# Hybrid attention block on one core: the first weight scale from ScalarE squares, first rows of x issued ahead of the constants

## The chip, the cores and the metric

The kernel runs on one core of one Trainium2 chip. The metric is the device time of one execution in microseconds; the time of a kernel is the median of its runs. PE is TensorE, DVE VectorE, ACT ScalarE, POOL GpSimd, and SP is SyncE, which here only issues transfers. Each engine works through its own queue of instructions in a fixed order.

## The reference

One layer of a residual block on x of 2048 rows by 1024 columns, in float32:

```
u  = rms_norm(x, norm1_w);  p = u @ w_in            # 1024 x 3072
diff q, k, v and sb q, k, v = columns of p
y_A: 4 heads, two softmax maps of normalised q and k, plus rel_bias by distance,
     chunk-causal, p0 - lam * p1, times v, rms_norm (diff_out_norm_w)
     lam = exp(sum(lambda_q1*lambda_k1)) - exp(sum(lambda_q2*lambda_k2)) + 0.2
y_B: 8 heads, stick-breaking attention, strictly causal, rms_norm (sb_out_norm_w)
h  = x + concat(y_A, y_B) @ w_out
out = h + SwiGLU(rms_norm(h, norm2_w); w_gate, w_up, w_down of width 2816)
```

## The kernel before, in words

**Number format.** Products are made in float16 at nearly float32 accuracy: each operand is scaled by a power of two and split into a high and a low half, and three matmuls (high-high, high-low, low-high) give one product. For a weight matrix the scale comes from its largest magnitude (or from sums of squares): a reduction per partition, a product with the identity that carries the 128 partial results across partitions (`across`, L177 and L178), then a few one-element DVE operations that cut the exponent out and write `sW` (L199). `split_weight` (L207 to L216) then makes the high half on ACT, DVE or POOL, whichever its running account of work finds least loaded, and the low half always on DVE (L215), from the raw weights and the high half.

**Work.** Rows of x go in 16 tiles of 128 rows. For each, `fresh` (L598) loads the rows into a `z4` buffer (nine of them), ACT squares and sums them (L220), POOL makes the reciprocal root (L151), DVE multiplies by root and gain (L223). `fresh_t` (L607) transposes the tile on PE in eight 128 x 128 pieces (L594), ACT casts each half of it to float16 (L612), DVE subtracts to get the low half (L613), and SP stores it for the later groups. The projection runs in eight groups of 384 columns (four of the differential heads, four of the stick-breaking ones); group 0 uses the tiles as they are made, the others read them back. Per group and tile PE makes 24 matmuls of 384 columns into `pj` (L320): eight blocks of 128 rows of weights, three matmuls each. `load_w` (L279) loads, scales and splits the weights of a group; for group 0 it is called at the start, for each other group at the ninth tile of the group before.

**Constants.** `gq`, `gk`, the four lambda vectors and the output gains (`mgain`) come by transfers on ACT's queue (L139, L680, L682) and are worked on by DVE in small steps (L650 to L690). `build_bias` (L625) makes the table of relative biases of four heads: a one-hot product on PE for each (L633), a copy on DVE (L635), a store and a skewed reload on POOL's queue (L637, L640), a last multiplication (L641).

**What sets the order.** The program is written as one sequence; a scheduler then fixes each engine's order by a timeline that it works out when the kernel is built, with priorities by part (`high_priority`), so a change at one place can move instructions anywhere behind it. Attention of group g runs beside the projection of group g+1. After attention come the output projection and the FFN, whose products run on PE almost without a break.

**Reading the names.** A reduction of the first weights is L187, the square of a later group's weights L184. In rows of order and profile, `wst` is a group's raw weights, `w` its two halves, `z` any row buffer, `xtr` a transposed half tile in PSUM, `xt` its float16 form, `wsc` the product that carries the scale across partitions, `xss` and `xrs` the sum of squares and reciprocal root of a row tile.

## Time and profile before

| | |
|---|---|
| median of 3 runs (2746.8 to 2756.92) | 2750.41 us |
| the profiled execution | 2752.86 us, span 2751.1 us |
| mean granted TensorE clock | 0.968 |
| PE busy | 2489.3 us, 90% of the span |
| DVE, ACT, POOL busy | 1967.9, 1357.8, 1428.8 us |
| first projection matmul | 25.40 us |

A row of the timeline gives start and length in us, engine, source line, operation, written from read tiles, shapes, how often in a row, and in brackets the engine's idle time before it with what ended that. Lengths in a chain overlap a little, so steps from start to start are the better measure. `SPq` and `ACTq` are the issuing of transfers by those engines. A single-pass PE transpose is counted once, a float32 matmul as two.

### The profile page before, as it was taken

What the parts mean: (1) busy time and instruction counts of PE and PEld (TensorE: products, weight loads), DVE (VectorE), ACT (ScalarE), POOL (GpSimd) and SP (SyncE); (2) the same over time, 40 slices, a digit from 0 to 9 for tenths busy, and PEclk for the clock granted to TensorE, in tenths of its full rate; (3) what the DMA queues carried; (4) which work ended last, traced back from release to release, by engine and by line L of the source; (5) the groups of instructions that cost most, each with busy time, mean ns of one, the idle gap of its engine ahead of it and who ended that gap; (6) DMA issues with size and microseconds to landing.
All of it is one profiled execution on the core that took longest, in us unless ns stands there. A gap on an engine that the chain in (4) does not pass through costs nothing.

```text
span 2751.1 us, 45381 instructions
## 1 busy us (share of the span) xinstructions
PE 2489.3 (90%) x17084; PEld 1411.3 (51%) x17084; DVE 1967.9 (72%) x3752; ACT 1357.8 (49%) x2539; POOL 1428.8 (52%) x1002
## 2 busy tenths in 40 slices
PE   7998989898878786788988899999999999999999
PEld 4655555555545453457775444444444444444444
DVE  6888879797989989977655878777776644443434
ACT  4665656566878778765644535353342211121120
POOL 2567767665454545546655656555654322232322
PEclk9999999999999997989999999999999999999999
DMA  7788787879999988987887665656657845535532
GB/s 231 197 163 182 151 191 160 180 167 206 196 209 194 199 177 150 205 186 202 211 247 271 235 232 192 225 204 213 237 200 280 339 150 187 210 131 199 188 118 93
DMA packets 646829, 543.52 MB, mean 198 GB/s; under 512 B 506368, under 2 KB 573952, under 8 KB 636368
## 3 DMA queue, kind: packets, MB, share of 16 engines
q1 hardware_dynamic: 644784, 538.53, 71.7%
q8 instruction: 134, 2.20, 0.3%
q0 software_dynamic: 512, 1.36, 0.2%
q14 instruction: 87, 0.71, 0.1%
q10 hardware_dynamic: 1312, 0.72, 0.1%
HBM read 261.08 MB, written 147.32 MB: 148 GB/s over the span
## 4 chain that ended last, share of the span: by engine, by line
PE 33%; DVE 7%; DMA 6%; POOL 3%; issue 3%; ACT 2%; SPq 0%; DVEq 0%; POOLq 0%; ACTq 0%
PE pd L1034 12%; PE pm L934 7%; PE pd L934 6%; PE pa L934 5%; DVE wd L215 2%; DMA stages<-in_w_down_dram 1%; DMA aT<-s 1%; POOL stages L98 1%; PE po L761 1%; POOL s L98 1%; DMA X<-xcd 1%; DMA stages<-in_w_up_dram 1%; DVE wu L215 1%; DVE cg L98 1%; DVE cg L999 1%
## 5 line engine op out<-in xcount | busy, mean ns | idle before, releaser
L98 POOL TENSOR_TENSOR s<-z,s 128x1024 f16<-128x1024 f32 (+7 forms) x288 | 473.5, 1652 | 339.3 <-ACT s L89 300.5
L320 PE MATMUL pj<-w,xt 128*128 128x384 f16 x3072 | 574.4, 335 | 28.1 <-DVE st L330 12.6
L320 PEld LDWEIGHTS <-xt 128*128 128x128 f16 x3072 | 300.7, 100 | 239.6 <-issue 39.4
L448 PE MATMUL sc<-kT,qT 128*128 128x512 f16 (+3 forms) x1280 | 346.8, 361 | 72.8 <-DVE z L558 32.1
L557 DVE TENSOR_TENSOR_SCAN z<-z,sc 128x512 f32<-128x512 f32 (+3 forms) x320 | 355.5, 1113 | 70.7 <-ACT sc L555 68.5
L1034 PE MATMUL pd<-wd,act 128*128 128x512 f16 x1764 | 392.9, 380 | 8.5 <-DVE cu L968 7.0
L458 PE MATMUL yp<-v,aT 128*128 128x64 f16 (+1 forms) x4896 | 281.0, 208 | 79.1 <-DMA aT<-s 78.4
L458 PEld LDWEIGHTS <-aT 128*128 128x128 f16 x4896 | 244.9, 102 | 169.1 <-DMA aT<-s 107.7
L934 PEld LDWEIGHTS <-wg 128*128 128x128 f16 x1848 | 181.3, 98 | 224.4 <-issue 10.9
L934 PEld LDWEIGHTS <-wu 128*128 128x128 f16 x1848 | 181.7, 98 | 220.8 <-issue 8.2
L98 POOL TENSOR_TENSOR act<-cg,act 128x512 f16<-128x512 f32 x109 | 150.4, 1390 | 259.4 <-ACT act L993 259.4
L1034 PEld LDWEIGHTS <-act 128*128 128x128 f16 x1764 | 172.8, 98 | 217.0 <-issue 10.9
L89 ACT CAST s<-z 128x384 f16<-128x384 f32 (+7 forms) x216 | 170.5, 790 | 157.8 <-DMA aT<-s 65.4
L98 POOL TENSOR_TENSOR stages<-stages 128x512 f32<-128x512 f32 x97 | 170.2, 1755 | 120.2 <-DVE wg L215 43.2
L98 POOL TENSOR_TENSOR hs<-hs,cu 128x512 f32<-128x512 f32 x102 | 132.6, 1306 | 162.0 <-DVE hs L1040 60.2
L554 ACT ACTIVATE z<-sc,c 128x512 f32<-128x512 f32 (+3 forms) x320 | 203.5, 636 | 10.7 <-PE sc L448 5.9
L558 DVE TENSOR_TENSOR z<-sc,z 128x512 f32<-128x512 f32 (+3 forms) x320 | 193.3, 606 | 8.1
L555 ACT ACTIVATE sc<-sc,c 128x512 f32<-128x512 f32 (+3 forms) x320 | 195.7, 611 | 0.0
L761 PE MATMUL po<-wo,mt 128*128 128x256 f16 x1536 | 182.4, 277 | 11.4 <-DVE xf L764 6.8
L993 ACT CAST act<-cg 128x512 f16<-128x512 f32 x126 | 76.8, 616 | 231.3 <-DVE cg L999 193.4
L1040 DVE SCALAR_TENSOR_TENSOR hs<-pd,c,hs 128x512 f32<-128x512 f32 x144 | 106.2, 747 | 116.8 <-PE pd L1034 104.5
L934 PE MATMUL pm<-X,wu 128*128 128x512 f16 x792 | 179.3, 379 | 1.8 <-ACT cg L979 1.7
(241 smaller groups left out, 4109.9 us busy)
## 6 DMA issues: line engine op xcount, KB each, us to landing
xt<-xs SPq DMA_DIRECT2D x112, 512.0 KB, 4.3
hs<-hd SPq DMA_DIRECT2D x72, 512.0 KB, 4.4
hd<-hs SPq DMA_DIRECT2D x56, 512.0 KB, 6.1
split<-wg SPq DMA_DIRECT2D x11, 1792.0 KB, 6.9
split<-wu SPq DMA_DIRECT2D x11, 1792.0 KB, 6.7
split<-wd SPq DMA_DIRECT2D x11, 1792.0 KB, 6.8
wg<-split SPq DMA_DIRECT2D x11, 1792.0 KB, 7.4
wd<-split SPq DMA_DIRECT2D x11, 1792.0 KB, 9.1
```

The costliest lines, as they stand in the source:

```text
L89: ACT.copy(dst, src)
L98: (DVE if e == "D" else POOL).tensor_tensor(dst, a_, b_, op)
L320: PE.matmul(pj[:, :384], lhsT=xv[:, xi, kt, :], rhs=G["w"][:, wi, kt, :], start=n == 0, stop=n == 23)
L448: PE.matmul(sc[:, : 128 * w].rearrange("p (t n) -> p t n", n=P), lhsT=G["q"][i // 4][:, 2 - 2 * o + m, i % 4, :], rhs=G["k"][q][:, m, 0:w, ...
L458: PE.matmul(yp[:, y0 : y0 + wd], lhsT=aT[:, a_, :], rhs=v[:, v_ : v_ + wd], start=start and j == 0 and q == 0, stop=stop and j == nb - 1 a ...
L554: ACT.activation(om[:, lo:hi], sc[:, :w], AF.Sigmoid, scale=G["nkz"][:])
L555: ACT.activation(sc[:, :w], sc[:, :w], AF.Sigmoid, scale=G["kz"][:])
L557: DVE.tensor_tensor_scan(ov, ov, sc[:, :w], om[:, hi : hi + 1], op0=ALU.mult, op1=ALU.bypass)
L558: DVE.tensor_tensor(be[:, lo:hi], sc[:, :w], om[:, lo + 1 : hi + 1], ALU.mult)
L761: PE.matmul(po[:, sl], lhsT=mt[:, kt, P * xi : P * xi + P], rhs=wos[2 * h + n][wi][:, kt, :], start=q == 0, stop=q == 23)
L934: PE.matmul(ps_[:].rearrange("p (t n) -> p t n", n=P), lhsT=wv[:, wo, wi, 128 * kt : 128 * kt + 128], rhs=X[xo][:, :, xi, kt, :], start=st ...
L1034: PE.matmul(po[:], lhsT=act[:, ao, xi, 128 * j : 128 * j + 128], rhs=W["d"][:, wo, wi, :], start=start and u == 0 and q == 0, stop=u == nu ...
```

## The change

Five edits, all in the start of the kernel and in `load_w`:

1. The scale of group 0's weights comes from three ACT squares with an accumulated sum, one for each third of the columns as it lands, in place of three DVE reductions of magnitudes (L187). DVE adds the three sums, one product carries them across partitions (instead of three).
2. Later groups' weights are squared in four pieces of 768 elements instead of one of 3072.
3. Loads of x, gain and weights, the norm of the gain row, row tile 0 and group 0's load are given high priority; row tile 1 is fed inside group 0's split, behind the scale.
4. High halves of group 0 are no longer made on DVE (`"AP"` for `"ADP"`); later groups' may also go to ACT.
5. The work on the constants is put in four functions that are emitted behind the first four projected tiles, queued behind the split and behind that tile's last projection matmul; the bias tables' buffers come from the tags `s16` and `aT` in place of `z4`. Group 1's load queues behind a copy of the ninth tile on ACT.

```diff
+            with tc.high_priority(4000):
+                SP.dma_start(xpre[0][:, :D], x[:P, :])
+                ACT.dma_start(w1[:, :D], a["norm1_w"].partition_broadcast(P))
+                st0 = fetch_w(0)
...
-            def load_w(g, st=None):
+            def load_w(g, st=None, hook=None):
...
+                junk = w16[:, : KT * 384].bitcast(BF16).rearrange("p (k n) -> p k n", k=KT)
                 if first:
-                    sW = weight_scale([st[:, :, 128 * j : 128 * j + 128] for j in range(3)], rW[:], pW[:], pt)
+                    pieces = [(st[:, :, 128 * j : 128 * j + 128], junk[:, :, 128 * j : 128 * j + 128]) for j in range(3)]
                 else:
-                    sW = weight_scale([st[:].rearrange("p k n -> p (k n)")], rW[:], pW[:], pt, w16[:, : KT * 384].bitcast(mybir.dt.bfloat16))
+                    pieces = [(st[:, 2 * j : 2 * j + 2, :], junk[:, 2 * j : 2 * j + 2, :]) for j in range(4)]
...
+                for j, (pc, jk) in enumerate(pieces):
+                    ACT.activation(jk, pc, AF.Square, accum_out=m0[:, j : j + 1])
+                note("A", 2900)
+                ms1 = sm.tile([P, 1], F32, tag="m1", name=nm("ms1"))
+                DVE.tensor_reduce(ms1[:], m0[:, : len(pieces)], op=ALU.add, axis=AX.X)
+                marks["scale"] = scale_end(lambda m: across(m, pt, [ms1[:]]), rW[:], pW[:], True, sW)
                 kn = 1 if first else 4
                 for k in range(0, KT, kn):
+                    if k == 3 and first:
+                        hook()
                     ks = slice(k, k + kn)
-                    split_weight(wv[:, 0, ks, :], wv[:, 1, ks, :], st[:, ks, :], 384 * kn, sW, "ADP" if first else "P")
+                    marks["split"] = split_weight(wv[:, 0, ks, :], wv[:, 1, ks, :], st[:, ks, :], 384 * kn, sW, "AP")
...
-                oh, rb = z4(), z4()
+                oh, rb = (s16p.tile([P, 2048], F16, tag="s16", bufs=SB, name=nm("oh"))[:].bitcast(F32) for _ in range(2))
...
-                    bt = z4()
+                    bt = sp.tile([P, 16, P], F16, tag="aT", bufs=AB, name=nm("bt"))[:].rearrange("p k n -> p (k n)").bitcast(F32)
...
+            later = (qk_gains, lambdas, build_bias, mix_gains)
...
-                        if g == 0 and t == 0:
-                            build_bias()
+                        if g == 0 and t < len(later):
+                            with tc.issue_after(first_split.ins), tc.issue_after(marks["proj"].ins):
+                                later[t]()
...
-                            Gs[g + 1] = load_w(g + 1)
+                            with tc.issue_after(marks["raw"].ins) if g == 0 else nullcontext():
+                                Gs[g + 1] = load_w(g + 1)
```

Line numbers of the changed kernel are a little higher: L627 and L628 there are L612 and L613 of before, L216 is L215, L299 the new square, L302 the new sum of its results.

ACT's queue from the first row tile's square on, before (`z_105`, `z_106` and `z_107` are the rows of tiles 0, 1 and 2; `wst_110` group 0's weights, `wst_813` group 1's):

```order
L220 ACTIVATE z_126,xss_127<-z_105 128x1024
L139 DMA lambda_q_238<-in_lambda_q_dram 128x64
L139 DMA lambda_k_240<-in_lambda_k_dram 128x64
L680 DMA c_265<-in_diff_out_norm_w_dram 128x1
L682 DMA c_265<-in_sb_out_norm_w_dram 64x1 x2
L220 ACTIVATE z_133,xss_134<-z_106 128x1024
L612 CAST xt_140<-xtr_141 128x512
L612 CAST xt_140<-xtr_148 128x512
```

and now:

```order
L220 ACTIVATE z_126,xss_127<-z_105 128x1024
L299 ACTIVATE w_149,m_154<-wst_110 128x8x128
L139 DMA lambda_q_225<-in_lambda_q_dram 128x64
L139 DMA lambda_k_227<-in_lambda_k_dram 128x64
L677 DMA c_229<-in_diff_out_norm_w_dram 128x1
L679 DMA c_229<-in_sb_out_norm_w_dram 64x1 x2
L299 ACTIVATE w_149,m_154<-wst_110 128x8x128 x2
L220 ACTIVATE z_174,xss_175<-z_106 128x1024
L627 CAST xt_133<-xtr_134 128x512
L627 CAST xt_133<-xtr_141 128x512
```

One square of the weights stands ahead of the remaining issues, two behind them and ahead of row tile 1's square and tile 0's casts.

DVE's queue around the first scale, before (`wsc` is what the product across partitions left; `sW` the scale):

```order
L178 TENSOR_REDUCE m_181<-wsc_175 128x1
L664 TENSOR_REDUCE c_242<-lambda_q_234 128x1
L654 TENSOR_SCALAR c_222<-c_222 128x1
L658 TENSOR_SCALAR c_230<-c_223 128x1
L663 TENSOR_TENSOR lambda_q_238<-lambda_q_238,lambda_k_240 128x64
L683 TENSOR_SCALAR c_265<-c_265 128x1
L133 TENSOR_SCALAR m_181<-m_181 128x1
L223 SCALAR_TENSOR_TENSOR z_133<-z_106,xrs_136,z_104 128x1024
```

and now, from the sum of the squares to the scale:

```order
L302 TENSOR_REDUCE ms_158<-m_154 128x1
L628 TENSOR_TENSOR xt_133<-xtr_134,xt_133 128x512
L178 TENSOR_REDUCE m_160<-wsc_152 128x1
L628 TENSOR_TENSOR xt_133<-xtr_141,xt_133 128x512
L195 TENSOR_SCALAR m_160<-m_160 128x1
L170 TENSOR_SCALAR c_151<-m_160 128x1
L171 TENSOR_SCALAR c_151<-c_151 128x1
L172 TENSOR_SCALAR c_150<-c_151 128x1
L130 TENSOR_SCALAR c_209<-c_151,c_118 128x1
L199 TENSOR_SCALAR sW_153<-c_150 128x1
```

The constants' operations and row tile 1's gain product are out of the scale's way; the two subtractions for tile 0 (`xt_133`) stand in it.

DVE's queue now from the split's second part to the end of tile 1's subtraction (`z_174`, `z_289`, `z_357` and `z_445` are the normalised rows of tiles 1 to 4, `xt_181` is tile 1 for the matmuls):

```order
L223 SCALAR_TENSOR_TENSOR z_174<-z_106,xrs_177,z_104 128x1024
L216 SCALAR_TENSOR_TENSOR w_149<-wst_110,sW_153,w_149 128x384 x3
L150 TENSOR_SCALAR xrs_449<-xss_447 128x1
L216 SCALAR_TENSOR_TENSOR w_149<-wst_110,sW_153,w_149 128x384
L684 TENSOR_TENSOR gk<-gk,gq 128x64
L694 TENSOR_TENSOR lambda_q_221<-lambda_q_221,lambda_k_223 128x64
L694 TENSOR_TENSOR lambda_q_225<-lambda_q_225,lambda_k_227 128x64
L645 COPY oh_410<-oh_410 32x512
L708 TENSOR_SCALAR c_229<-c_229 128x1
L223 SCALAR_TENSOR_TENSOR z_289<-z_107,xrs_292,z_104 128x1024
L223 SCALAR_TENSOR_TENSOR z_357<-z_356,xrs_361,z_104 128x1024
L628 TENSOR_TENSOR xt_181<-xtr_182,xt_181 128x512
```

Behind that stand L223 of `z_445`, two small reductions and tile 1's second half. Before, tile 1's subtractions stood ahead of the split. On PE, the first projection matmuls now have eight transposes (tile 0) ahead of them instead of sixteen transposes and two bias products; from there on transposes stand up to four tiles ahead of the projection, where before they stood one tile ahead.

95 lines of the change are left out of this document (51 added, 44 removed).

## The prediction

> **What bounds the kernel now.** I read the page's 40 slices first, then the busy times by stage, then the timeline of the first 46 us, where the change puts its instructions. The view by stage gives the busy us of PE, PEld, DVE, ACT and POOL (instruction counts in brackets), the granted TensorE clock, the DMA share and GB/s:
>
> ```profile
> 0.00:25.40 25.40, 9.66 (x29) 6.33 (x30) 15.68 (x53) 8.88 (x15) 6.33 (x15) 1.00 0.61 187
> ...
> 39.90:43.40 3.50, 0.01 (x1) 0.00 (x0) 0.44 (x2) 3.50 (x8) 0.92 (x2) 1.00 0.69 260
> 43.40:105.00 61.60, 58.48 (x373) 38.59 (x374) 50.69 (x83) 36.59 (x79) 27.50 (x24) 0.94 0.70 220
> ```
> ```profile
> 105.00:1550.00 1445.00, 1236.35 (x11175) 823.66 (x11174) 1185.14 (x2603) 950.52 (x1971) 859.53 (x582) 0.95 0.86 194
> ```
> ```profile
> 1550.00:2751.00 1201.00, 1170.31 (x5451) 535.58 (x5449) 708.24 (x988) 356.46 (x467) 529.98 (x372) 0.99 0.56 200
> ```
>
> PE is the engine to watch. It loses 15.7 us ahead of its first projection, 3.5 us at 40 us, 3.1 us in the rest of the first projection pass, 208.7 us in the attention stages and 30.7 us in the FFN. The change works on the first three losses, 22.3 us in all. From about 1600 us on every engine has the same order in both programs, so that an early lead passes through there and nothing new arises.
>
> The start, on PE:
>
> ```profile
> 16.32 0.79 PE L177 MATMUL wsc<-id,m 128*128 128x128 f32 x2 [1.49 <-DVE c L133]
> 17.58 1.97 PE L594 MATMUL xtr<-id,z 128*128 128x128 f32 x8 [0.46 <-DVE z L223]
> ...
> 25.40 2.45 PE L320 MATMUL pj<-w,xt 128*128 128x384 f16 x7
> ...
> 33.80 0.91 PE L633 MATMUL bt<-z,z 32*128 32x384 f32 x2
> 34.64 4.40 PE L320 MATMUL pj<-w,xt 128*128 128x384 f16 x26
> 38.87 1.04 PE L594 MATMUL xtr<-id,z 128*128 128x128 f32 x8
> 43.45 2.82 PE L320 MATMUL pj<-w,xt 128*128 128x384 f16 x8 [3.54 <-ACT xt L612]
> ```
>
> A projection matmul steps by (38.87 - 34.64) / 26 = 0.163 us, a transpose takes 1.04 / 8 = 0.13 us, one bias table's product 34.64 - 33.80 = 0.84 us. At 43.45 us two row tiles are projected (48 matmuls) and three transposed (24). The 3.54 us stall is ACT's: it waits for group 1's weights and squares them whole, ahead of the casts:
>
> ```profile
> 38.59 2.76 ACT L184 ACTIVATE w<-wst 128x3072 bf16<-128x3072 f32 x1 [3.14 <-DMA wst<-in_w_in_dram]
> ...
> 41.35 0.36 ACT L341 ACTIVATE raw<-pj 128x256 f32<-128x256 f32 x1
> ...
> 42.81 1.07 ACT L612 CAST xt<-xtr 128x512 f16<-128x512 f32 x2
> ```
>
> **Step 1: the first scale, some 1.1 us earlier.** Three DVE reductions of the weights go, three ACT squares come. On ACT, the issues of 12 to 15 us and two squares:
>
> ```profile
> 13.84 1.17 ACTq L682 DMA_DIRECT2D c<-in_sb_out_norm_w_dram  x2
> ```
> ```profile
> 44.03 1.08 ACT L220 ACTIVATE z<-z 128x1024 f32<-128x1024 f32 x1
> ...
> 45.07 1.08 ACT L220 ACTIVATE z<-z 128x1024 f32<-128x1024 f32 x1
> ```
>
> The new order puts the second and third square behind the sb_out transfers, whose issue ends at 15.01 us. A square of 1024 elements with its accumulator read steps by 45.07 - 44.03 = 1.04 us, so the sums are there at 17.1. But DVE's new queue holds the subtraction for tile 0's first half ahead of the scale's last reduction, and ACT makes that half's cast only after squaring row tile 1 (18.1) and casting for 1.07 / 2 us (18.7). The DVE rows for what follows:
>
> ```profile
> 16.25 1.27 DVE L223 SCALAR_TENSOR_TENSOR z<-z,xrs,z 128x1024 f32<-128x1024 f32 x1
> ```
> ```profile
> 22.36 0.67 DVE L613 TENSOR_TENSOR xt<-xtr,xt 128x512 f16<-128x512 f32 x1
> ...
> 29.14 0.27 DVE L178 TENSOR_REDUCE c<-msc 128x1 f32<-128x128 f32 x1
> ...
> 29.45 0.56 DVE L635 COPY z<-bt 128x384 f32<-128x384 f32 x1
> 29.93 0.14 DVE L133 TENSOR_SCALAR c<-c 128x1 f32<-128x1 f32 x1
> ...
> 30.11 0.15 DVE L134 TENSOR_SCALAR c<-c 128x1 int32<-128x1 int32 x1
> ```
>
> A subtraction of 0.67 us, a reduction of 0.27, the second subtraction and five dependent small operations at 30.11 - 29.93 = 0.18 us: 18.7 + 2.5 = 21.2 is the scale's end. Before, by the first row here, it was 22.1:
>
> ```profile
> 21.99 0.13 DVE L199 TENSOR_SCALAR sW<-c 128x1 f32<-128x1 f32 x1
> ```
> ```profile
> 22.22 3.08 POOL L214 TENSOR_SCALAR w<-wst,sW 128x384 f16<-128x384 f32 x4 [3.73 <-DVE sW L199]
> ```
> ```profile
> 23.80 1.13 DVE L215 SCALAR_TENSOR_TENSOR w<-wst,sW,w 128x384 f16<-128x384 f32 x2
> ```
> ```profile
> 23.92 1.38 POOL L214 TENSOR_SCALAR w<-wst,sW 128x384 f16<-128x384 f32 x1
> ```
> ```profile
> 28.61 0.60 DVE L215 SCALAR_TENSOR_TENSOR w<-wst,sW,w 128x384 f16<-128x384 f32 x1
> ```
>
> Row tile 0 itself is ready earlier, but PE can do nothing with it ahead of the weights.
>
> **Step 2: the split, some 1.7 us of loss.** Before, POOL and ACT made four high halves each; now POOL makes seven. POOL's first three took (23.92 - 22.22) / 3 = 0.57 us each. Its fourth took 1.38 us beside two low halves on DVE, and ended 0.37 us behind them. So I let POOL's high halves take turns with DVE's low halves and with the gain product of row tile 1 (L223) that now stands among them: 7 x 0.57 + 8 x 0.57 + 1.27 = 9.8 us, ending at 31.0. Were they side by side, DVE alone would set the end: 0.8 for the first high half, 8 x 0.57 and 1.27 give 6.6 us and 27.8. Before it was 29.2. I take 31.0, as the 1.38 us row is the nearest one, and keep 27.8 for the range.
>
> The Trainium skill speaks against this edit: "SBUF — State Buffer", section "SBUF: two separate sides", says that a VectorE operation with two SBUF inputs and a GpSimd operation that reads SBUF exclude each other on a shared port pair, for the whole instruction. The rows above agree (1.38 against 0.57 us); by that rule the split ends at the later of my two values, without it at the earlier.
>
> **Step 3: tiles 0 to 2.** Behind the last low half DVE's new queue holds five constant operations (1.2 us), the L223 of row tiles 2 and 3, the first half of tile 1's subtraction, another L223, two small reductions (0.4) and the second half: 31.0 + 1.2 + 3 x 1.27 + 2 x 0.67 + 0.4 = 37.7. PE needs that half from tile 1's fifth block on and has ten matmuls left, so tile 1 ends at 39.3. Before it ended at about 39.0: up to here nothing is won.
>
> What is won lies behind. No square of group 1 stands on ACT here any more (they come some eight row tiles later, when those weights have long landed), so that the 3.54 us go; and at 39.3 PE has done 36 transposes where it had done 24. Lead: (43.45 - 39.3) + 12 x 0.13 = 5.7 us. Against it stand the four bias products and the mgain one (as the 0.79 us row), which lay ahead of 43 us and now come later: 4 x 0.84 + 0.8 = 4.2. That leaves 1.5 us.
>
> **Step 4: rest of the pass.** PE's waits between 43 and 105 us (engine, tile, line, releaser: total, times, longest):
>
> ```profile
> PE wsc L177 <- ACT raw L341: 1.6, 1, 1.6
> PE xtr L594 <- DVE xt L613: 0.8, 1, 0.8
> PE pj L320 <- DVE m L178: 0.6, 1, 0.6
> ```
>
> All are at the spot where group 1's scale is formed; it moves behind the ninth tile's projection, with its sum formed beforehand. Between none and all of 3.0 us go; I take two thirds, 2 us. The constants that move into this stage (four bias copies of 0.56 us, some twenty small operations of 0.14) cost DVE 5 us, under 61.6 - 50.7 = 10.9 us of its idle time. If that cover fails, PE waits for DVE and these 2 us are lost with the lead.
>
> **Step 5: later groups.** Each group's one square, 41.35 - 38.59 = 2.76 us to the next, becomes four of 768 elements. The nearest row is an exponential of that size, which steps by 0.92 us:
>
> ```profile
> 127.24 0.93 ACT L497 ACTIVATE z<-z,ng 128x768 f32<-128x768 f32 x1
> ...
> 128.16 0.92 ACT L497 ACTIVATE z<-z,ng 128x768 f32<-128x768 f32 x1
> ```
>
> ACT gains 4 x 0.92 - 2.76 = 0.9 us of work a group, 6.4 us over seven. It is busy 950.5 of the 1445 us of these stages, so I cost this at nothing; without that cover it is 6.4 us. Of the six sets that fall there four stand in one piece on ACT, so that little comes in between. One large high half moves from POOL to ACT: nothing.
>
> **The sum.** -1.5 - 2 = -3.5 us on the profiled execution (2752.86 us for a span of 2751.1, and 2.5 us above the median of 2750.41). On the median: **2747 us**. With the side-by-side split (31.0 - 27.8 = 3.2) and all of step 4's waits it is -1.5 - 3.2 - 3.0 = -7.7; with the DVE cover failing, 0.
>
> **The rivals.** Up to 1550 us all orders were drawn anew, mostly by a few places, and the trace cannot price that exactly. PE's longest waits there:
>
> ```profile
> PE yp L458 <- DMA aT<-s: 78.4, 66, 4.2
> PE sc L448 <- DVE z L558: 32.1, 34, 2.0
> ```
>
> - *Slower, through SP's queue.* PE's value products wait for transposing transfers, which SP issues in order; the first such moves stand at the first batches (k's transpose ahead of q's, an attention transpose ahead of a q one). The place is the 78.4 us row: a fifth more there is +15.7, and 2747 becomes 2762. From 5% more on, the lead is gone. For it: 66 waits, each hanging on one neighbour in a queue. Against: the moves are short and go both ways.
> - *Faster.* The lead of 7.7 us, and 15% less of the same wait (-12): 2750.4 - 7.7 - 12 = 2731.
> - *The change doesn't do what it says.* The scale comes no earlier, as the squares stand behind ACT's issues and the cast, and DVE's constants eat steps 3 and 4: 2750. For it: step 3 wins nothing up to tile 1.
>
> **How the numbers follow.** Forecast 0.50 (2747, own range 2743 to 2750); no lead 0.16 (2750); slower 0.16 (2762); faster 0.18 (2731). A measurement of this kernel can tell about 0.5%, 13.8 us, from no change. Below 2736.7 lies the faster rival alone, 0.18; above 2764.2 half of the slower one, 0.08; the rest, 0.74, is no change. The range reaches to both outer cases and leaves out half of each, 0.17: 2731 to 2760.
>
> **What would show it.** Step 1: two squares starting at 15 us on ACT, and the scale at 21 us on DVE. Step 2: POOL's high halves at 1.1 to 1.4 us each between DVE's low ones, the last of which ends at 31 us. Step 3: tile 1's end at 39 us with no 3.5 us gap behind it. Step 4: the first attention scores some 4 us earlier than in this row:
>
> ```profile
> 104.73 0.34 DVE L487 CUSTOM_DVE_ANT_0 z<-sc,bias,c 128x128 f32<-128x128 f32 x1
> ```
>
> Rival: PE's wait for aT well off 78 us. I would be wrong if the split ended by 28 us, if the transposes that now stand up to four tiles ahead held PE up for late rows of x, or if the attention stages differed by more than 10 us.

## The result, and the profile after

| | before | changed |
|---|---|---|
| median, run beside each other | 2752.18 us (2744.71 to 2756.92, 22 runs) | 2756.15 us (2752.87 to 2762.55, 22 runs) |
| ratio of changed to before | | 1.0020, 95% interval 1.0012 to 1.0028 |
| the same on another occasion | | 1.0025, 1.0015 to 1.0035 |
| the profiled execution | span 2751.1 us | span 2759.8 us |
| mean granted TensorE clock | 0.968 | 0.968 |

The changed kernel is slower by 0.2%, some 5 to 7 us, where 3.5 us less were forecast. The profiled execution of the changed kernel lies 5.4 us over its median, so that the two profiles differ by more (8.7 us) than the kernels do. Up to 45 us its profile does nearly what the forecast says. DVE's timeline, from the scale on:

```profile
21.12 0.15 DVE L199 TENSOR_SCALAR sW<-c 128x1 f32<-128x1 f32 x1
...
24.31 0.94 DVE L216 SCALAR_TENSOR_TENSOR w<-wst,sW,w 128x384 f16<-128x384 f32 x1
25.18 1.60 DVE L223 SCALAR_TENSOR_TENSOR z<-z,xrs,z 128x1024 f32<-128x1024 f32 x1
26.70 0.94 DVE L216 SCALAR_TENSOR_TENSOR w<-wst,sW,w 128x384 f16<-128x384 f32 x1
27.56 0.93 DVE L216 SCALAR_TENSOR_TENSOR w<-wst,sW,w 128x384 f16<-128x384 f32 x1
28.42 0.60 DVE L216 SCALAR_TENSOR_TENSOR w<-wst,sW,w 128x384 f16<-128x384 f32 x1
...
29.01 0.60 DVE L216 SCALAR_TENSOR_TENSOR w<-wst,sW,w 128x384 f16<-128x384 f32 x1
```

The scale is there at 21.3 us (22.1 before), and the last low half ends at 29.6 (29.2 before, 31.0 forecast). POOL's high halves beside that:

```profile
21.45 2.01 POOL L214 TENSOR_SCALAR w<-wst,sW 128x384 f16<-128x384 f32 x3 [11.89 <-DVE c L130]
23.43 0.85 POOL L151 TENSOR_TENSOR xrs<-xrs,mh 128x1 f32<-128x1 f32 x1
24.27 0.58 POOL L214 TENSOR_SCALAR w<-wst,sW 128x384 f16<-128x384 f32 x1
24.83 0.88 POOL L214 TENSOR_SCALAR w<-wst,sW 128x384 f16<-128x384 f32 x1
25.68 1.55 POOL L214 TENSOR_SCALAR w<-wst,sW 128x384 f16<-128x384 f32 x1
27.21 0.88 POOL L214 TENSOR_SCALAR w<-wst,sW 128x384 f16<-128x384 f32 x1
```

The two engines take turns here. A POOL half takes 0.58 us alone or first, and 0.88, 1.55 and 0.88 us where it starts beside a low half, the gain product (L223) and another low half. DVE's low half takes 0.60 us alone and 0.94 or 0.93 us beside POOL, the gain product 1.60 us where it took 1.27 alone. Read by their ends, each of POOL's last three halves ends 0.45 us after the DVE instruction that it met; each of DVE's three low halves beside them ends 0.40 us after POOL's half, and the gain product 1.07 us after (25.71 to 26.78). The second profile of the changed kernel has the same steps.

PE's timeline from the last matmuls of row tile 1 on has no gap at the place of the old 3.54 us, and row tile 3's projection starts at 45.2 us, where the two profiles of the kernel before have 50.0 and 51.8:

```profile
36.34 2.11 PE L335 MATMUL pj<-w,xt 128*128 128x384 f16 x12
38.29 0.60 PE L609 MATMUL xtr<-id,z 128*128 128x128 f32 x4
38.72 1.46 PE L335 MATMUL pj<-w,xt 128*128 128x384 f16 x8
...
43.70 1.55 PE L648 MATMUL bt<-oh,oh 32*128 32x384 f32 x4
45.19 0.99 PE L335 MATMUL pj<-w,xt 128*128 128x384 f16 x5
```

At 50 us PE has made 88 projection products and 60 transposes (73 and 32 before). At 80 us it has made 209 and 96 (213 and 96). The whole lead goes in these 30 us, in which PE is idle for 4.7 us and was idle for none before. The waits of PE between 43 and 105 us (engine, tile, line, releaser: total, times, longest):

```profile
PE xtr L609 <- DVE xt L628: 4.2, 3, 1.7
PE wsc L177 <- DVE ms L302: 2.2, 1, 2.2
PE pj L335 <- DVE c L178: 1.3, 1, 1.3
```

That is 7.7 us, where before had 6.5 us with the 3.5 us gap, and 3.0 without it (in a second profile of each, 7.2 us against 10.5 with a gap of 7.7, so 2.8 without it). The transposes wait for PSUM that DVE has not read out yet, and POOL's timeline shows why DVE is late:

```profile
55.35 0.59 POOL L655 DMA_DIRECT2D bias<-bd  x1 [2.49 <-DMA bd<-bt]
55.93 0.54 POOL L652 DMA_DIRECT2D bd<-bt  x1
57.50 0.54 POOL L655 DMA_DIRECT2D bias<-bd  x1 [1.03 <-DMA bd<-bt]
58.06 0.57 POOL L151 TENSOR_TENSOR xrs<-xrs,mh 128x1 f32<-128x1 f32 x1
61.60 0.59 POOL L655 DMA_DIRECT2D bias<-bd  x1 [2.97 <-DVE xrs L150]
62.20 0.56 POOL L151 TENSOR_TENSOR xrs<-xrs,mh 128x1 f32<-128x1 f32 x1
```

POOL issues the bias tables' transfers, and reading a table back waits for the landing of its write. POOL stands still meanwhile, and the power that finishes a row tile's reciprocal root stands behind it. DVE's next gain products then wait:

```profile
58.66 1.28 DVE L223 SCALAR_TENSOR_TENSOR z<-z,xrs,z 128x1024 f32<-128x1024 f32 x1 [2.20 <-POOL xrs L151]
...
62.80 1.28 DVE L223 SCALAR_TENSOR_TENSOR z<-z,xrs,z 128x1024 f32<-128x1024 f32 x1 [1.67 <-POOL xrs L151]
```

and PE with them, 1.68 us at 64.9 and 1.75 us at 71.7. Before, the tables were read back between 28 and 42 us, and the power behind the last of these reads, at 43.0 us, waited for DVE and not for the read. The rest goes at group 1's scale: its squares, held behind the ninth tile's copy, stand on ACT from 82.9 to 86.3 us, and PE waits 2.21 us for their sum.

From 105 us to the end of the projections PE's longest wait is the one for the attention's transposing transfers, as before:

```profile
PE yp L473 <- DMA aT<-s: 87.4, 78, 3.4
PE sc L463 <- DVE z L573: 30.2, 41, 1.5
```

The first row was 78.4 us, in 66 times. To place the loss, marks that every kernel here has were read from the timelines: the first attention score on PE, the first of the 320 scans on DVE (the stick-breaking half begins), the 241st, the last. Two profiles of one program differ too, which shows how much a difference has to be:

| us | first score | first scan | 241st | last | 241st to last | last scan to end |
|---|---|---|---|---|---|---|
| before | 104.3 | 614.4 | 1135.2 | 1400.3 | 265.1 | 1350.8 |
| before, second profile | 106.4 | 613.8 | 1135.4 | 1396.8 | 261.4 | 1349.6 |
| changed | 106.4 | 614.4 | 1134.4 | 1404.6 | 270.2 | 1355.2 |
| changed, second profile | 108.8 | 617.3 | 1137.2 | 1404.7 | 267.5 | 1352.5 |

At the 241st scan the kernels are level within what repeats differ. In the last group's attention, with the output projection beginning under it, the changed kernel takes 268.9 us on the mean of its two profiles, the other 263.3: 5.6 us more. The repeats of one kernel differ by 2.7 and 3.7 us there, so that two profiles of each make this the likely place and don't prove it. Behind the last scan the changed kernel's profiles take another 3.7 us more on the mean (repeats 2.7 and 1.2 us apart); no wait was found for these. PE's waits from the 241st to the last scan, changed kernel:

```profile
PE yp L473 <- DMA aT<-s: 17.9, 10, 3.4
PE osc L177 <- ACT wo L184: 5.0, 3, 2.7
PE po L789 <- DVE xrs L150: 3.3, 2, 2.2
```

and kernel before:

```profile
PE yp L458 <- DMA aT<-s: 12.5, 13, 2.2
PE po L761 <- DVE xf L764: 6.8, 6, 3.3
PE sc L448 <- DVE z L558: 5.3, 6, 1.7
```

5.4 us more for aT, and 5.0 us at a place that was free of waits: the product that carries the output weights' scale across partitions (`osc`) comes up in PE's queue before the squares that it needs are done. The second profiles have the same: 17.3 us against 11.7 for aT, 4.1 against none at `osc`. No edit touches these operations; their places in the queues were drawn anew.

### The profile page after: what moved, and what is told of

The parts are those of the page before. It is cut to its first block, busy times and chain, and to the rows that moved or that the text cites. A ratio compares the mean times of both kernels' runs of the same rounds, so it can differ in the third digit from the quotient of the medians.

```text
span 2759.8 us, 45460 instructions
## 1 busy us (share of the span) xinstructions
PE 2485.6 (90%) x17080; PEld 1408.3 (51%) x17080; DVE 1979.1 (72%) x3761; ACT 1363.4 (49%) x2580; POOL 1438.7 (52%) x1006
## 4 chain that ended last, share of the span: by engine, by line
PE 35%; DVE 8%; DMA 5%; issue 3%; POOL 3%; ACT 2%; SPq 0%; DVEq 0%; POOLq 0%; ACTq 0%
PE pd L1062 14%; PE pm L962 8%; PE pd L962 6%; PE pa L962 5%; DVE wd L216 2%; PE po L789 2%; DMA aT<-s 1%; DMA stages<-in_w_down_dram 1%; DVE wu L216 1%; DMA X<-xcd 1%; POOL stages L98 1%; POOL s L98 1%; DVE cg L1027 1%; DVE cg L98 1%; DVE z L572 1%
## 5 line engine op out<-in xcount | busy, mean ns | idle before, releaser
L335 PE MATMUL pj<-w,xt 128*128 128x384 f16 x3072 | 569.2, 333 | 17.9 <-ACT raw L356 6.0
L473 PE MATMUL yp<-v,aT 128*128 128x64 f16 (+1 forms) x4896 | 283.1, 209 | 88.4 <-DMA aT<-s 87.4
L789 PE MATMUL po<-wo,mt 128*128 128x256 f16 x1536 | 185.7, 280 | 11.7 <-DVE c L172 3.8
L1068 DVE SCALAR_TENSOR_TENSOR hs<-pd,c,hs 128x512 f32<-128x512 f32 x144 | 106.3, 748 | 115.5 <-PE pd L1062 109.4
L962 PE MATMUL pm<-X,wg 128*128 128x512 f16 x792 | 181.6, 383 | 1.2 <-ACT bx L1137 1.2
```

Source lines behind the costliest of these rows:

```text
L335: marks["proj"] = PE.matmul(pj[:, :384], lhsT=xv[:, xi, kt, :], rhs=G["w"][:, wi, kt, :], start=n == 0, stop=n == 23)
L473: PE.matmul(yp[:, y0 : y0 + wd], lhsT=aT[:, a_, :], rhs=v[:, v_ : v_ + wd], start=start and j == 0 and q == 0, stop=stop and j == nb - 1 a ...
L789: PE.matmul(po[:, sl], lhsT=mt[:, kt, P * xi : P * xi + P], rhs=wos[2 * h + n][wi][:, kt, :], start=q == 0, stop=q == 23)
L962: PE.matmul(ps_[:].rearrange("p (t n) -> p t n", n=P), lhsT=wv[:, wo, wi, 128 * kt : 128 * kt + 128], rhs=X[xo][:, :, xi, kt, :], start=st ...
```

## The experiments

All ratios are to the kernel before, run beside the kernel in question. The theories in the expectations: **A**, the deferred constants eat the lead; **B**, the redrawn order decides; **C**, the longer squares in pieces are on the path; **D**, the front wins and other parts lose it; **E**, queues of engines that issue transfers hold the first pass up, and what is won there reaches the end.

| | ratio, 95% interval | first score | first scan | last scan | 241st to last |
|---|---|---|---|---|---|
| e1 constants early | 1.0034, 1.0022 to 1.0045 | 109.2 | 618.8 | 1402.9 | 264.2 |
| e2 one square later | 1.0050, 1.0038 to 1.0063 | 108.1 | 619.7 | 1407.9 | 267.1 |
| e3 only pieces | 1.0028, 1.0016 to 1.0040 | 108.6 | 615.0 | 1402.7 | 263.2 |
| e4 redraw only | 0.9998, 0.9987 to 1.0009 | 107.2 | 626.5 | 1404.1 | 255.5 |
| e6 front only | 1.0027, 1.0016 to 1.0038 | 111.1 | 618.2 | 1397.5 | 255.4 |
| e7 deferral only | 1.0023, 1.0013 to 1.0032 | 112.0 | 623.2 | 1396.5 | 253.4 |
| e8 bias buffers only | 0.9987, 0.9974 to 1.0000 | 104.1 | 609.7 | 1388.7 | 257.1 |
| e9 bias reads held | 1.0031, 1.0019 to 1.0043 | 106.3 | 610.4 | 1404.0 | 267.2 |
| e10 group 1 not held | 1.0020, 1.0007 to 1.0032 | 107.4 | 617.0 | 1398.4 | 254.5 |
| e11 changed, redrawn | 1.0057, 1.0043 to 1.0072 | 107.1 | 626.7 | 1406.9 | 254.6 |
| e12 before again | 1.0001, 0.9992 to 1.0010 | 106.4 | 613.8 | 1396.8 | 261.4 |
| e13 start delayed | 1.0018, 1.0009 to 1.0028 | 109.0 | 615.4 | 1396.9 | 262.6 |
| e14 group 1 later | 0.9994, 0.9983 to 1.0004 | 94.7 | 611.7 | 1384.8 | 251.6 |
| e15 wo earlier | 1.0009, 0.9999 to 1.0019 | 106.0 | 610.6 | 1395.1 | 263.2 |
| e16 bias buffers again | 0.9978, 0.9967 to 0.9989 | 104.5 | 618.4 | 1397.7 | 255.2 |
| e17 front and buffers | 0.9969, 0.9955 to 0.9982 | 105.2 | 613.6 | 1386.3 | 254.7 |
| e18 both repairs | 1.0016, 1.0001 to 1.0030 | 94.2 | 610.8 | 1399.7 | 261.9 |

**e1**, from the changed kernel:

```diff
-            later = (qk_gains, lambdas, build_bias, mix_gains)
+            for part in (qk_gains, lambdas, mix_gains):
+                part()
...
-                        if g == 0 and t < len(later):
-                            with tc.issue_after(first_split.ins), tc.issue_after(marks["proj"].ins):
-                                later[t]()
+                        if g == 0 and t == 0:
+                            build_bias()
```

> The changed kernel, with its deferred constants and bias tables put back to where the kernel before has them (the small constant products straight behind group 0's weights, the bias tables behind the first row tile's projection); all else stays changed. In the changed kernel PE waits 7.7 us between 43 and 105 us (transposes for DVE's subtraction 4.2, group 1's scale product 2.2, the mgain slot 1.3), and a lead of 15 projection products and 28 transposes at 50 us is gone at 80. Theory A (the deferred work fills DVE, POOL and the projection's slots in the first pass, and that eats the lead): PE's waits in 43 to 105 us fall to 4 us or less, the first attention scores start 3 to 4 us before the changed kernel's 106.4 us, and the time is 3 to 4 us under the changed kernel's, about the kernel before's 2752. Theory B (the time is made by how the order from 1130 us on was redrawn, where the changed kernel loses 5 us): the time stays at the changed kernel's, some 4 to 5 us over the kernel before, whatever the first scores do.

A falls as it was put: PE's waits between 43 and 105 us are 11.4 us, not 4 or less, and nothing is won in the time. Tile 8 starts at 75.4 us, 2 us sooner, and then another queue takes over. SP's timeline:

```profile
70.33 1.34 SPq L387 DMA_TRANSPOSE qT<-st  x1
...
72.34 1.57 SPq L387 DMA_TRANSPOSE kT<-st  x1
74.02 1.43 SPq L389 DMA_DIRECT2D qT<-qT  x2
75.54 0.54 SPq L629 DMA_DIRECT2D xs<-xt  x1
76.12 0.45 SPq L618 DMA_DIRECT2D z<-in_x_dram  x1
```

The last row tile's load is issued behind the first q and k transposes, and ACT, in order too, stands still for it:

```profile
82.04 1.06 ACT L220 ACTIVATE z<-z 128x1024 f32<-128x1024 f32 x1 [3.80 <-DMA z<-in_x_dram]
```

Tile 9 starts at 90.1 us, 3 us later than in the changed kernel.

**e2**, from the changed kernel:

```diff
-                    pieces = [(st[:, 2 * j : 2 * j + 2, :], junk[:, 2 * j : 2 * j + 2, :]) for j in range(4)]
+                    pieces = [(st[:].rearrange("p k n -> p (k n)"), w16[:, : KT * 384].bitcast(BF16))]
```

> The changed kernel, with one square over all 3072 elements for the weights of groups 1 to 7, as before, in place of four pieces of 768. Theory C (the pieces' longer work, 3.4 us by the rows at 82.9 to 86.3 us against 2.76 for one square, lies on the path of every group): 5 to 6 us under the changed kernel, at or below the kernel before's 2752. Theories A and B: no gain that follows the number of groups; the first pass as in the changed kernel (first scores at 106 us give or take 1), and the time within 3 us of the changed kernel's 2756, but for what a new order draws at 1130 to 1280 us.

**e3** does the converse: the kernel before with only the four pieces and DVE's sum of them, for groups 1 to 7.

```diff
-                    sW = weight_scale([st[:].rearrange("p k n -> p (k n)")], rW[:], pW[:], pt, w16[:, : KT * 384].bitcast(mybir.dt.bfloat16))
...
+                    for j in range(4):
+                        ACT.activation(junk[:, 2 * j : 2 * j + 2, :], st[:, 2 * j : 2 * j + 2, :], AF.Square, accum_out=m0[:, j : j + 1])
...
+                    DVE.tensor_reduce(ms1[:], m0[:], op=ALU.add, axis=AX.X)
```

> The kernel before, with only the squares of groups 1 to 7 in four pieces and their sum formed by DVE. Theory C: 5 to 6 us over the kernel before, so 1.002 of it. Theory A: no change at the start, and the time of the kernel before. Theory B: the order of all engines up to 1500 us is redrawn by this edit too, so the time may move by some 5 us either way, with the difference arising at few places and not by an equal step in each group.

Taking the pieces out costs, and putting them in costs: 1.0050 against the changed kernel's 1.0020 to 1.0025, and 1.0028 against 1. C would need opposite signs. It falls as a term that adds up; what both edits share is a redrawn order.

**e4**, from the kernel before, changes only the planner's tally:

```diff
+            note("A", 300)
             ahead, nq, nx = [], [], [0, 0]
```

> The kernel before, with 300 ns added once to the planner's tally of ACT ahead of the first row tiles: no instruction is added or left out but one or two small ones that change their engine, and the order of every engine is redrawn (403 places on DVE against 518 in the changed kernel). Theory B: a time off the kernel before's by 2 to 8 us, of either sign. Theories A and C: the time of the kernel before within 2 us, since none of the work that they blame is there.

The time stays, where B had 2 to 8 us. Inside, the profile is 12 us later at the first scan and takes 6 to 10 us less from the 241st to the last. How much of that is the order isn't shown: this profile is of an execution of 2759.66 us, 11 us over the run's median of 2748.50, and two profiles of another program (e8 and e16) are 8.7 us apart at the first scan. What e4 does show is that not every draw changes the time.

**e5 and e12** are the two kernels unaltered, for the second profiles of the table above; e5's ratio is the 1.0025.

> The changed kernel once more, unaltered, as the yardstick for the other three on the same chip and for how far two profiled executions of one program differ, stage by stage. All theories: 1.001 to 1.003 of the kernel before. If the 5 us that the first profile loses between 1130 and 1300 us belong to the order (theory B), they stand here too; if they are the chance of one execution, they don't.

> The kernel before, unaltered, for a second profile of it: how far two executions of one program differ, stage by stage, next to the 1 to 3 us between the two profiles of the changed kernel. All theories: ratio 1.000, first scores within 1 us of 104.7 us. Theory B needs the stage from 1135 to 1400 us to come out within 3 us of the first profile's 265 us; where it doesn't, the 4 to 5 us lost there by the changed kernel are within chance.

The loss stands in the second profile of the changed kernel too (267.5 us). But the second profile of the kernel before has 261.4 us, 3.7 off the first one's 265.1: by the condition set here, the 4 to 5 us lost in this stage are within chance. What both profiles of each kernel do share are the waits for aT and at `osc`.

**e6**, from the changed kernel, leaves only the front (edits 1 and 3 and the `"AP"` of group 0); it is e17 below with the old buffers:

```diff
-                oh, rb = (s16p.tile([P, 2048], F16, tag="s16", bufs=SB, name=nm("oh"))[:].bitcast(F32) for _ in range(2))
+                oh, rb = z4(), z4()
...
-                    bt = sp.tile([P, 16, P], F16, tag="aT", bufs=AB, name=nm("bt"))[:].rearrange("p k n -> p (k n)").bitcast(F32)
+                    bt = z4()
```

**e7**, from the kernel before, makes only the deferral:

```diff
-                        if g == 0 and t == 0:
-                            build_bias()
+                        if g == 0 and t < len(later):
+                            with tc.issue_after(first_split.ins), tc.issue_after(marks["proj"].ins):
+                                later[t]()
```

**e8**, from the kernel before, makes only the new buffers, and **e16** is e8 once more:

```diff
-                oh, rb = z4(), z4()
+                oh, rb = (s16p.tile([P, 2048], F16, tag="s16", bufs=SB, name=nm("oh"))[:].bitcast(F32) for _ in range(2))
...
-                    bt = z4()
+                    bt = sp.tile([P, 16, P], F16, tag="aT", bufs=AB, name=nm("bt"))[:].rearrange("p k n -> p (k n)").bitcast(F32)
```

Expected of e6, e7, e8 and e16, in this order:

> The changed kernel reduced to its front: group 0's weights and row tile 0 ahead of all else, their scale from ScalarE squares, high halves on ACT and POOL, the second row tile within the split. The constants, bias tables, their buffers, and the later groups' weights are as in the kernel before. Theory D (the front is worth what it wins, and the other parts lose it again): tile 1 of the projection done at 39 us or before, the first attention scores 2 to 4 us before the kernel before's 104.7 us, and 0.998 to 0.999 of its time. Theory B (the lead doesn't last, since the order behind it is redrawn): a lead at 50 us, nothing left of it by 130 us, and a time between the kernel before's and 8 us over it.

> The kernel before, with only the constant products and the bias tables held back to the first four row tiles' projections. Theory A's remainder (deferral by itself costs DVE and PE in the first pass): 2 to 4 us over the kernel before, first scores 2 us later than 104.7 us. Theory D: the same, since the deferral is one of the parts that lose. Theory B: as the other redrawn orders, 0 to 8 us over the kernel before, without a link to the first scores.

> The kernel before, with only the bias tables' buffers changed (from the pool of row buffers to those of the attention's fp16 scores and transposes); no operation is added, dropped or moved in the program text. Theories A and D: the kernel before's time within 2 us. Theory B: the order is redrawn by this as well (512 places on DVE), and the time is 0 to 8 us over the kernel before.

> The kernel before with only the bias tables' buffers changed, once more, on another occasion. Its first ratio was 0.9987, from 0.9974 to 1.0000. Theory B: 0.998 to 1.000 again, as a property of its order, with the profile within 3 us of its first one up to 1300 us. If the first result was chance: 0.9995 to 1.001.

Front alone and deferral alone are each as slow as the whole change, with first scores 5 to 8 us late. D falls in this form. The buffers alone are a gain, twice, which no theory had for e8. In the kernel before, the bias build takes six of the nine row buffers (two inputs and four tables). The order there puts the fourth row tile's load on SP behind group 1's weights, which wait for the end of the split, and the next two loads wait for the bias tables' product and store. SP's timeline and waits there:

```profile
29.29 2.90 SPq L266 DMA_DIRECT2D wst<-in_w_in_dram  x3
32.29 2.79 SPq L603 DMA_DIRECT2D z<-in_x_dram  x2
```
```profile
SPq L266 <- DVE w L215: 4.9, 1, 4.9
...
SPq L603 <- DMA bd<-z: 1.3, 1, 1.3
SPq L603 <- PE bt L633: 0.6, 1, 0.6
```

With buffers of their own (e8):

```profile
15.42 10.02 SPq L603 DMA_DIRECT2D z<-in_x_dram  x4
```

Row loads start 17 us sooner and tile 9 starts at 81.2 us (81.7 in the second profile), where before has 85.4 and 87.0. What of the 0.2% comes from there and what from the stage behind the 241st scan, shorter by 4 to 10 us (but 1 to 4 us longer behind the last scan), isn't settled: the first scans, at 609.7 and 618.4 in two profiles of one program, don't tell.

**e9** moves the reading back of the tables behind the last row tile's power on POOL:

```diff
-                    skew = bass.AP(tensor=ap.tensor, offset=ap.offset + 127, ap=[[383, P], [1, 256]])
-                    POOL.dma_start(bias[:, h, :], skew)
+                    skews.append(bass.AP(tensor=ap.tensor, offset=ap.offset + 127, ap=[[383, P], [1, 256]]))
+
+            def read_bias():
+                with tc.issue_after(pows[-1].ins):
+                    for h in range(4):
+                        POOL.dma_start(bias[:, h, :], skews[h])
...
+            later = {0: qk_gains, 1: lambdas, 2: build_bias, 3: mix_gains, 14: read_bias}
```

> The changed kernel, with the four DMAs that read the bias tables back (bias<-bd) queued on POOL behind the last row tile's power, in place of between the powers of earlier row tiles. In the changed kernel they wait there for the four writes (bd<-bt), 2.5, 1.0 and, behind a power, 0.6 us, and the powers of two row tiles stand behind them: DVE's L223 waits 2.2 and 1.7 us for those, PE's transposes 4.2 us for DVE. Theory E (POOL's queue is what eats the lead in the first pass): these waits of DVE and PE fall under 1.5 us, row tile 8's projection starts 3 us before the changed kernel's 77.4 us, the first attention scores 2 to 3 us before its 106.4 us, and the time is 2 to 3 us under the changed kernel's, if the order behind does not undo it. Theory B (the order behind decides): the lead at the first scores shows or not, and the time is within 0 to 8 us over the kernel before either way.

The mechanism shows: DVE's wait for the powers goes from 5.4 to 2.1 us, PE's wait for the subtraction from 4.2 to 1.7, and tile 8 starts at 75.5 us. PE's waits between 43 and 105 us in e9:

```profile
PE pj L337 <- DVE c L180: 2.6, 1, 2.6
PE wsc L179 <- DVE ms L304: 2.2, 1, 2.2
PE xtr L611 <- DVE xt L630: 1.7, 1, 1.7
```

But the two others eat the 2 us: tile 9 starts at 86.7 us (86.9 changed), and the time isn't better.

**e10** takes the hold off group 1's load:

```diff
-                            with tc.issue_after(marks["raw"].ins) if g == 0 else nullcontext():
+                            with nullcontext():
```

> The changed kernel, with group 1's weights no longer queued behind the raw copies of ScalarE: their squares may stand wherever the planner puts them. In the changed kernel they stand at 82.9 to 86.3 us, and PE waits 2.2 us for their sum at 86.5. Theory E: this hold is a second, smaller part of the loss; PE's wait at the scale product falls under 1 us, the first scores start 1 to 2 us earlier than 106.4 us. Theory B: whatever the first scores do, 0 to 8 us over the kernel before.

Its squares go back to the third tile (tile 3 starts at 50.0 us, tile 9 again at 86.7): group 1's squares cost PE some 4 us at either place, and the time, 1.0020, is the changed kernel's. **e14** puts that load behind the twelfth tile, on top of e9:

```diff
-                        if t == PF and g + 1 < NG:
+                        if t == (11 if g == 0 else PF) and g + 1 < NG:
```

> The kernel with the bias reads held on POOL, and with group 1's weights loaded and scaled behind the twelfth row tile's projection in place of the ninth's. With the reads held the changed kernel won 2 us up to tile 8 and lost them at group 1's squares, 82.9 to 86.3 us. Theory E: tile 9's projection starts at 82 to 84 us in place of 86.7, the first scores come 2 to 4 us before 106.4 us, and the time is 2 to 4 us under the changed kernel's. Theory B: a lead at the first scores, and a time anywhere from the kernel before's to 14 us over it, the span of the redrawn orders so far.

Now the lead stays in the first pass: tile 9 starts at 79.5 us, the first scores at 94.7. PE's waits between 43 and 105 us that are over 0.7 us are one:

```profile
PE pj L337 <- DVE c L180: 1.5, 1, 1.5
```

The time is 0.9994, by the ratios about 10 us under e9. But the two don't hang together as E has it: at the first scan e14 is at 611.7 us, e9 at 610.4. Of 11.6 us at the first scores nothing is left by then, and what is won arises for the most part behind the 241st scan (251.6 us against 267.2 in the two profiles, of which some 3 us go again behind the last scan).

**e11** is the redraw of e4 in the changed kernel:

```diff
+            note("A", 300)
             ahead, nq, nx = [], [], [0, 0]
```

> The changed kernel, with 300 ns added once to the planner's tally of ACT ahead of the first row tiles, as was done to the kernel before in an earlier run: the work stays the same, the order of all engines is redrawn. Theory B: a time that may leave the changed kernel's by up to 8 us, toward the kernel before or away. Theory E: the first pass has the same POOL waits, and the time is the changed kernel's within 2 us, 1.0015 to 1.003 of the kernel before.

1.0057: with the same work, but for two small operations that change their engine, 0.3% (some 9 us) over the changed kernel. This is the clearest price of an order alone.

**e13** delays the start of the changed kernel:

```diff
+                SP.dma_start(xpre[0][:, :D], x[P : 2 * P, :])
                 SP.dma_start(xpre[0][:, :D], x[:P, :])
```

> The changed kernel, with one more load at its head: another row tile of x goes into row tile 0's buffer and is then overwritten, so that row tile 0, and the weights queued behind it on SP, come later by one such transfer (issue to landing 5.6 us). Nothing else is altered, and the order behind is nearly the changed kernel's (180 of DVE's 3507 instructions change their place, against 1254 from before to changed). Theory E (what is won or lost at the start reaches the end): first scores 4 to 6 us after the changed kernel's 106.4 us, and a time 4 to 6 us over the changed kernel's, 1.0035 to 1.005 of the kernel before. Theory B (the order behind absorbs it or decides): first scores later by as much, but the time within 2 us of the changed kernel's, 1.0015 to 1.003.

Row tile 0's square starts at 16.9 us in place of 7.6. The weights are not delayed, as was expected: their first square starts at 10.3 us (10.5 in the changed kernel) and their scale is there at 19.4 (21.3). Tile 3 starts at 48.7 us in place of 45.2. At tile 8 it is 78.2 against 77.4 and 78.5 in the two profiles of the changed kernel, at tile 9 89.5 against 86.9 and 88.3, and the time isn't longer (1.0018). So most of the 3.5 us at the fourth row tile is swallowed within five tiles; the waits of the pass shrink in return, DVE's for the powers from 5.4 to 2.9 us, PE's for the subtraction from 4.2 to 1.7.

**e15** loads the output weights a tile earlier in the changed kernel, **e18** in e14:

```diff
-WT = (4, 7, 10)
+WT = (3, 6, 9)
```

Expected of e15, then of e18:

> The changed kernel, with the output projection's weights loaded one row tile earlier in the last group (behind its tiles 3, 6 and 9 in place of 4, 7 and 10). The order of all engines is the changed kernel's up to some 1100 us. Theory B: up to 1095 us the profile follows the changed kernel's within 3 us; from 1135 to 1400 us it differs by 3 us or more, either way, and the time with it; if PE's 5.0 us wait for the squares of these weights is the cause, it shrinks and the time falls by up to 5 us. Theory E: no difference over 2 us.

> The changed kernel with bias reads held, group 1 three row tiles later, and the output weights one row tile earlier. If the repairs add (10 us by the first, 4 us by the second, against the changed kernel's 1.0025): 0.997 to 0.999 of the kernel before. Theory B: the last group's order is redrawn again by the first repair, so the second repair does not carry over: 0.9985 to 1.002.

The same edit on the last group wins in one (1.0009, `osc` waits 3.0 us for 5.0, 263.2 us for 268.9) and loses in the other (1.0016 against 0.9994, 261.9 us for 251.6, with 1.8 us at `osc` where there was no wait). Up to some 1020 us each has its parent's order. The intervals overlap in both pairs, the second by little, so that this is a hint and no proof: the edit's worth isn't its own, but that of the queue it falls into.

**e17** is the front together with the bias buffers: from the changed kernel, the deferral, the hold and the later groups' `"AP"` are undone, and those groups' weights are squared whole again:

```diff
-            later = (qk_gains, lambdas, build_bias, mix_gains)
+            for part in (qk_gains, lambdas, mix_gains):
+                part()
...
-                            with tc.issue_after(marks["raw"].ins) if g == 0 else nullcontext():
+                            with nullcontext():
...
-                    marks["split"] = split_weight(wv[:, 0, ks, :], wv[:, 1, ks, :], st[:, ks, :], 384 * kn, sW, "AP")
+                    marks["split"] = split_weight(wv[:, 0, ks, :], wv[:, 1, ks, :], st[:, ks, :], 384 * kn, sW, "AP" if first else "P")
```

> The front alone, as in the run of that name (constants, order of the bias tables and later groups as in the kernel before), together with the bias tables' new buffers. Theory E (the front wins its 2 to 4 us where nothing gives them back): 0.9965 to 0.9980 of the kernel before, under the bias buffers alone. Theory B (a start that is earlier by some us is swallowed by the first pass, and the order behind decides): not under the bias buffers alone, 0.998 to 1.003.

This beats both kernels: 0.9969, some 8.5 us under the kernel before. Against the buffers alone (0.9978, 0.9987) the intervals overlap, so the front's own share isn't settled. Where the gain arises isn't settled either. In its profile the last scan comes 12 us before the mean of the kernel before's two (1386.3 us against 1398.6), but from there to the end it takes 1357.8 us against 1350.2, so that 7.6 of the 12 us are given back. PE's waits from the 241st to the last scan:

```profile
PE yp L476 <- DMA aT<-s: 8.7, 8, 2.2
PE sc L466 <- DVE z L576: 7.2, 8, 1.7
PE po L792 <- DVE xf L795: 6.7, 9, 1.8
```

8.7 us for aT, where before had 12.5 and the changed kernel 17.9, and no row for `osc`.

## Why the prediction was wrong

**Step 1 held.** 21.2 us was forecast for the scale's end, 21.3 came.

**Step 2 held in kind, too large in size.** 31.0 us forecast, 29.6 measured, 0.4 us later than before instead of 1.7. POOL's halves and DVE's work did take turns, as forecast. What was too large is a turn: the sum took 0.57 us for each half and 1.27 for the gain product, their whole lengths alone, where a turn added 0.45 us (POOL's half), 0.40 (DVE's low half) and 1.07 (the gain product). The recorded lengths of neighbours overlap by the rest, 0.13 to 0.20 us. The rule of the Trainium skill that was weighed there ("SBUF — State Buffer", section "SBUF: two separate sides": the one that starts first keeps the shared port pair for the whole instruction, the other is blocked) agrees with this trace, up to that overlap.

**Step 3 held.** The gap is gone, tile 1's end lies at 38 us (39.3 forecast), and tile 3 starts 4.8 us sooner, with 28 transposes more done at 50 us. The bias products come behind that, as charged.

**Step 4 failed, and with it the sign at the first scores.** It took 2 of 3.0 us of PE's waits off the rest of the pass and let the constants cost DVE 5 us under 10.9 us of its idle time. PE's waits there went from 3.0 to 7.7 us (2.8 to 7.2 in the second profiles). The cover on DVE was counted; the queue that the moved step issues on wasn't: four reads of the bias tables, each waiting on POOL for a write to land, ahead of the powers that DVE waits for. e9 shows this mechanism, and that taking it away alone only uncovers group 1's squares, which the step had rightly seen as moved but not as standing between two tiles with nothing beside them. The first scores, forecast 4 us sooner, came 2 us later. This alone doesn't give the time its sign: without these waits e9 is still at 1.0031.

**Step 5's term is no term.** The four squares step by 0.82 us and take 3.4 us in place of 2.76, 0.7 us more a group, as worked out (0.9). But e2 and e3 show that they don't add up to anything that goes by groups.

**The sum is what failed for the time.** It put the redrawn orders up to 1550 us at nothing, and passed an early lead on to the end. Neither holds. e11 shows that a redrawn order of the same work can cost some 9 us (and e4 that it can cost nothing). e13 and e14 show that 3.5 us at the fourth tile and 11.6 us at the first scores don't reach the first scan; and the changed kernel's loss is read in the last group, 5.6 us, and behind it, 3.7 us, as far as two profiles of each can tell. The rival for that was named, more waiting for aT through the queue of SP, at 78.4 us; it went to 87.4, 5.4 of these 9.0 us in the last group, which is less than the 15.7 priced. It got 0.16, and the forecast 0.50. That 2756 us lies inside 2731 to 2760 is owed to the width that this rival gave the range, and not to the sum.

**What stays open**: why the last group falls into about 252 to 257 us in some orders and 262 to 270 in others. Over all 20 profiles the wait at `osc` goes with it. The nine that have 1.8 us or more there (the changed kernel's two, e1, e2, e3, e9, e13, e15, e18) take 261.9 to 270.2 us; of the eleven with 0.2 us or less, nine take 251.6 to 257.1, and the other two are the kernel before's. The wait for aT doesn't sort them: 8.4 us in e3 with 263.2, 14.7 us in e6 with 255.4. This goes together and is not shown to be the cause, since 2 to 5 us at `osc` are less than the difference and no run moves that wait alone. Which edit at the start leads to which order is not explained by anything in the edit.

## What to carry to other kernels

When a step is moved that issues transfers, look at what stands behind its issue on that engine's queue: a transfer that waits for another one (2.49 us on POOL here) holds up the engine's arithmetic too, and whoever waits for that. Where a scheduler fixes the order, measure a redraw without any change of work beside the change (here 0 and 9 us), and test the parts alone and in pairs, since they need not add: front alone +0.27%, buffers alone -0.13 and -0.22%, both -0.31%. A start some us earlier or later need not reach the end: here 3.5 us at the fourth tile and 11.6 us at the first scores did not reach the first scan.

## What the runs showed of the hardware

- Two profiles of one program can differ by 8.7 us at 614 us (609.7 and 618.4 in e8 and e16) with the same order of instructions, while their medians, of 12 runs each, agree within 0.1% of each other. A stage of a single profile is no measure of a few us here; repeats are.
- POOL's high half (128x384) reads one fp32 operand from SBUF, DVE's low half that one and a second. Alone they took 0.58 and 0.60 us. Beside each other they took turns: POOL's half ended 0.45 us after DVE's instruction, DVE's half 0.40 us after POOL's. A mean over four POOL halves, 0.96 us, hides this; the single rows (0.58, 0.88, 1.55, 0.88) show it.
- A square of 3072 elements with an accumulated sum takes 2.76 us on ACT, four of 768 elements 0.82 us each from start to start.
